# Renumbering the slots of the expert tables in a mixture-of-experts layer

## The chip, the cores and the metric

The kernel runs on one core of a Trainium2 chip. The metric is the device time of one execution, in microseconds (us); lower is better. The kernel before takes 911.71 us as the median of three runs (911.01 to 913.59). One execution was recorded by the hardware profiler; it took 911.96 us, and its span from the first to the last instruction is 909.6 us. A second measurement of this kernel would be told from no change at about 0.3%, that is 2.7 us.

The core has five engines that matter here. PE multiplies matrices, ACT (ScalarE) and DVE (VectorE) work element by element, POOL (GpSimd) issues the indirect transfers, and SP issues the plain transfers. All transfers are carried out by 16 DMA engines, whoever issues them.

## The reference

One decoder layer on 1024 tokens of width 1024: a layer norm, two kinds of attention side by side, an output projection, a layer norm, a mixture of experts, and a last layer norm. The change concerns the experts only.

```python
def hierarchical_moe(h, w_group, b_group, w_router, b_router, w_gate, w_up, w_down):
    ...
    g_top, g_idx = lax.top_k(group_probs, 1)          # 1 of 4 groups
    ...
    e_top, e_idx = lax.top_k(in_group, TOP_K)         # 2 of the 8 experts in it
    weights = g_top * jax.nn.softmax(e_top, axis=-1)
    expert_ids = g_idx * EXPERTS_PER_GROUP + e_idx
    ...
    hid = silu(xb @ w_gate[e]) * (xb @ w_up[e])       # 1024 -> 256
    hid = hid * combine
    out = sum over e of hid @ w_down[e]               # 256 -> 1024
```

Each token goes to two of 32 experts. An expert's weights are three blocks of 1 MB (gate, up and down, 128 partitions of 8 KB each).

## The kernel before

**The tables.** While the router runs, the kernel builds for each expert a list of its tokens. `route` (line 1475) counts with a triangular matrix how many earlier tokens chose the same expert; that count `pos` is the token's rank in the expert. Line 1529 compares `pos` with the row of constants `iota`, which gives a one-hot row of 128 columns, and the product in line 1533 puts the token's number into the list, on the partition whose `iota` equals the rank:

```python
                V.tensor_scalar(O, iota, pos[:, b, k:k + 1], None, op0=OP.is_equal)
                ...
                PE.matmul(flat(T), O, flat(Vk), start=(n == 0 and k == 0), stop=(n == NB - 1 and k == 1))
```

`finish_table` (line 1375) adds 4096 to each entry. An entry that holds a token becomes its number from 0 to 1023. An empty one becomes 4096, which is out of bounds for the indirect transfers, and they skip it. With `iota` equal to the column number, an expert with n tokens has its rows on partitions 0 to n-1. `overflow_table` (line 1820) uses the same `iota` for tokens of rank 128 and above, which go to an extra tile.

**The expert stage.** 33 tiles run one after the other (line 1878): 32 experts and, as tile 24, the overflow tile. The rows of each tile, counted by running the routing of the reference on its inputs, are in the order of the tiles 66, 74, 17, 76, 35, 58, 13, 55, 80, 79, 48, 22, 93, 123, 47, 67, 71, 62, 60, 25, 128, 121, 51, 68, 4 (overflow), 83, 96, 35, 70, 64, 93, 29, 35: 2048 rows of 4 KB in all. For each tile

- `gather_x` (line 1656) fetches its rows from the tensor `h_d` in device memory by an indirect DMA on POOL's queue (`w<-h_d,idx` in the trace), four tiles ahead;
- `load_chunk` (line 1328) fetches the three 1 MB blocks by plain DMAs on SP's queue (`rw<-in_w_e_dram`), each as soon as one of some ten buffers is free (`rw` has eight); tile 24 fetches its blocks by an indirect DMA;
- `w_split` (line 1551) turns each half block into a high and a low part, one operation on ACT (`whg`, `whd`) and one on DVE (`wlg`, `wld`), and so frees the buffer;
- PE transposes the rows (`x_tr`), multiplies (`gate_up`, `down`), and for tiles 0 to 30 `scatter` (line 1715) adds the result to the rows of `y_d` by an indirect DMA that accumulates (`y_d<-w,idx`).

All 128 rows of a tile are computed, whatever their number; an empty row holds old data and is multiplied by zero. After tile 30 all rows of `y_d` are read back for the last layer norm (`norm_rows`, `rw<-y_d`). Tiles 31 and 32 are not accumulated: their rows are fetched from `y_d` (`old_rows`, `w<-y_d,idx`), added, normalised and written into the output by an indirect DMA (`renorm`, `out_dram<-w,idx`), the last thing that the kernel does.

The order of all instructions is worked out ahead of time by a planner in the kernel (`Sched`, line 201), which knows shapes but not the numbers in a table.

Of the kernel before, what the change touches and what calls it, by code (L numbers as in the profile page):

```python
# [37 lines left out]
C_ID, C_TRI, C_IOTA, C_E32 = 0, 128, 256, 384  # L38
# [1932 lines left out]
def _constants():  # L1971
    import numpy as np
    c = np.zeros((128, C_END), np.float32)
    q = np.arange(128)[:, None]
    k = np.arange(128)[None, :]
    c[:, C_ID:C_ID + 128] = np.eye(128)
    cur = np.where(k <= q, 0.0, NEG)
    mask = np.concatenate([(k > q) & (k >= 128 - NMETA), cur, q > k, q <= k], axis=1).astype(np.float32)
    c[:, C_TRI:C_TRI + 128] = q < k
    c[:, C_IOTA:C_IOTA + 128] = k  # L1980
    col = np.arange(512)[None, :]
    bd = ((q[:64] // NMETA) == (col // 128)).astype(np.float32)
    c[:, C_E32:C_E32 + 32] = np.arange(32)
    J, e = np.divmod(np.arange(224), 32)
    key = np.zeros((128, 2, 7, 32), np.float32)
    key[:, 0] = (32 * (J + 1) + e).reshape(7, 32)
    key[:, 1] = (128 * (J + 1)).reshape(7, 32)
    c[:, C_TOK:C_TOK + 8] = np.arange(128)[:, None] + 128 * np.arange(8)[None, :] - EMPTY
    c[:, C_WROW] = 3 * np.arange(128)
    inv = 10000.0 ** (-np.arange(0, 64, 2, dtype=np.float32) / np.float32(64))  # L1990
    pos = np.zeros((128, 9), np.float32)
    pos[:, :8] = NMETA + 128 * np.arange(8)[None, :] + np.arange(128)[:, None]
    pos[:, 8] = np.maximum(np.arange(128) - (128 - NMETA), 0)
    ang = (pos[:, :, None] * inv.astype(np.float32)[None, None, :]).astype(np.float32)
    rope = np.zeros((128, 9, 2, 64), np.float32)
    rope[:, :, 0, :32] = rope[:, :, 0, 32:] = np.cos(ang)
    rope[:, :, 1, :32] = -np.sin(ang)
    rope[:, :, 1, 32:] = np.sin(ang)
    return c, rope, bd, key, mask
# [51 lines left out]
```

## Time and profile before

| | us |
|---|---|
| median of three runs | 911.71 |
| the profiled execution | 911.96 |
| its span, first to last instruction | 909.6 |
| first scatter to the last one (tiles 0 to 30) | 534.9 to 846.2 |
| PE busy in the span | 804.9 (88%) |
| DVE, ACT busy | 683.5 (75%), 512.9 (56%) |
| transfers on POOL's queue | 28.87 MB, 12816 packets |
| transfers on SP's queue | 166.41 MB, 36688 packets |

Up to about 505 us the kernel runs attention and the router, from there to about 846 us the expert stage, and then the tail with the last layer norm. In the views of DMA queues, q1 is SP's queue and q0 is POOL's; a share is the time that the queue's packets took, as a share of 16 DMA engines' time in the stretch. A row that a tile gathers or scatters is one packet of 4 KB, a row of a weight block one packet of 8 KB; very small packets go with them. "To landing" is the time from the issue of a transfer until all 16 DMA engines have reported that their part is done.

### The profile page before, as it was taken

What the parts mean: (1) busy time and instruction counts of PE and PEld (TensorE: products, weight loads), DVE (VectorE), ACT (ScalarE), POOL (GpSimd) and SP (SyncE); (2) the same over time, 40 slices, a digit from 0 to 9 for tenths busy, and PEclk for the clock granted to TensorE, in tenths of its full rate; (3) what the DMA queues carried; (4) which work ended last, traced back from release to release, by engine and by line L of the source; (5) the groups of instructions that cost most, each with busy time, mean ns of one, the idle gap of its engine ahead of it and who ended that gap; (6) DMA issues with size and microseconds to landing.
All of it is one profiled execution on the core that took longest, in us unless ns stands there. A gap on an engine that the chain in (4) does not pass through costs nothing. (4 is left out here: it accounts for less than half of the span.)

```text
span 909.6 us, 13571 instructions
## 1 busy us (share of the span) xinstructions
PE 804.9 (88%) x4616; PEld 688.2 (76%) x4616; DVE 683.5 (75%) x1379; ACT 512.9 (56%) x966; POOL 312.9 (34%) x561
## 2 busy tenths in 40 slices
PE   3899999999999999999998499999899989998520
PEld 3898998999999988888887388888677767765410
DVE  7946623888777655658667799998897779878595
ACT  3524322576665635512122598998787768768541
POOL 3757423344331215232214324343332243332100
PEclk9999999999999999999999699999999999999855
DMA  9544512121211112799957477999999999996632
GB/s 335 175 145 169 167 67 94 46 87 55 85 50 47 48 70 70 241 354 397 348 172 281 151 264 226 349 374 363 335 343 353 321 332 366 353 347 209 197 133 104
DMA packets 49574, 196.14 MB, mean 216 GB/s; under 512 B 12689, under 2 KB 14225, under 8 KB 37345
## 3 DMA queue, kind: packets, MB, share of 16 engines
q1 hardware_dynamic: 36688, 166.41, 49.3%
q0 software_dynamic: 12816, 28.87, 11.5%
q8 instruction: 37, 0.61, 0.3%
q14 instruction: 33, 0.26, 0.1%
HBM read 165.57 MB, written 49.05 MB: 236 GB/s over the span
## 5 line engine op out<-in xcount | busy, mean ns | idle before, releaser
L312 DVE TENSOR_TENSOR wlg<-rw,whg 128x1024 fp32r<-128x1024 f32 x120 | 143.3, 1220 | 32.4 <-ACT whg L312 32.1
L312 POOL DMA_INDIRECT y_d<-w,idx x33 | 72.4, 2193 | 224.6 <-ACT w L312 180.4
L312 ACT ACTIVATE whg<-rw 128x1024 fp32r<-128x1024 f32 x120 | 124.5, 1060 | 42.5 <-DMA rw<-in_w_e_dram 37.2
L312 PE MATMUL sc<-wh,ht 128*128 128x448 f32 (+3 forms) x400 | 116.2, 371 | 1.9 <-DVE ht L312 1.3
L312 PE MATMUL gu<-wlg,xh 128*128 128x512 f32 x264 | 106.3, 403 | 10.4 <-DVE wlg L312 10.4
L312 PE MATMUL gu<-whg,xh 128*128 128x512 f32 x264 | 109.3, 414 | 2.8 <-ACT whg L312 2.8
L312 PE MATMUL gu<-whg,xl 128*128 128x512 f32 x264 | 104.9, 398 | 2.1 <-DVE xl L312 2.1
L312 PEld LDWEIGHTS sc<-wh,ht 128*128 128x128 f32 x400 | 74.3, 192 | 9.5 <-DVE ht L312 1.8
L312 PE MATMUL sc<-wl,ht 128*128 128x448 f32 (+3 forms) x200 | 73.1, 365 | 0.0
L312 PEld LDWEIGHTS gu<-wlg,xh 128*128 128x128 f32 x264 | 49.9, 189 | 28.7 <-DVE wlg L312 18.1
L312 DVE TENSOR_TENSOR wld<-rw,whd 128x1024 fp32r<-128x1024 f32 x58 | 68.3, 1220 | 2.1 <-ACT whd L312 2.1
L312 PEld LDWEIGHTS gu<-whg,xh 128*128 128x128 f32 x264 | 50.0, 190 | 13.4 <-ACT whg L312 4.8
L312 PEld LDWEIGHTS gu<-whg,xl 128*128 128x128 f32 x264 | 50.2, 190 | 12.8 <-DVE xl L312 4.0
L312 ACT ACTIVATE whd<-rw 128x1024 fp32r<-128x1024 f32 x58 | 58.3, 1059 | 0.3 <-PE y L312 0.3
L312 PE MATMUL y<-whd,hh 128*128 128x512 f32 x124 | 51.3, 414 | 0.0
L312 PE MATMUL sc<-w,oT 128*128 128x512 f32 x192 | 49.8, 402 | 0.6 <-DMA oT<-o_d 0.6
L312 PE MATMUL tr<-cs,w 128*128 128x128 f32 x264 | 40.4, 277 | 10.9 <-DMA w<-h_d,idx 7.3
L312 DVE TENSOR_TENSOR xl<-tr,xh 128x512 fp32r<-128x512 f32 x66 | 45.2, 685 | 6.4 <-ACT xh L312 6.1
L312 ACT ACTIVATE pt<-sc,ng 128x272 f32<-128x272 f32 (+9 forms) x56 | 29.8, 538 | 34.5 <-DVE ng L312 34.3
L312 PE MATMUL y<-wld,hh 128*128 128x512 f32 x124 | 49.1, 396 | 0.0
L312 PE MATMUL y<-whd,hl 128*128 128x512 f32 x124 | 49.0, 395 | 0.0
L312 POOL DMA_INDIRECT w<-h_d,idx x33 | 44.1, 1337 | 11.2 <-issue 5.5
(331 smaller groups left out, 1961.3 us busy)
## 6 DMA issues: line engine op xcount, KB each, us to landing
rw<-in_w_e_dram SPq DMA_DIRECT2D x88, 1024.0 KB, 20.7
o_d<-oT SPq DMA_DIRECT2D x16, 512.0 KB, 2.7
oT<-o_d POOLq DMA_DIRECT2D x16, 512.0 KB, 8.5
x<-in_w_in_dram SPq DMA_DIRECT2D x8, 672.0 KB, 6.3
u_d<-r SPq DMA_DIRECT2D x7, 672.0 KB, 3.3
h_d<-h SPq DMA_DIRECT2D x8, 512.0 KB, 3.2
hr<-h_d SPq DMA_DIRECT2D x8, 512.0 KB, 9.7
h_d<-hr SPq DMA_DIRECT2D x8, 512.0 KB, 4.5
```

The costliest lines, as they stand in the source:

```text
L312: inst = getattr(t.eng.real, method)(*[self.real(a) for a in args], **{k: self.real(v) for k, v in kw.items()})
```

## The change

The row of constants `iota` gets other numbers. Column k held k; it now holds k % 8 * 16 + k // 8. So the token of rank r, which stood on partition r, stands on partition 8 * (r % 16) + r // 16: ranks 0 to 15 on partitions 0, 8, 16, ... 120, ranks 16 to 31 on partitions 1, 9, 17, ... 121, and so on. 64 rows, for example, stood on partitions 0 to 63 and stand now on those 64 partitions whose number leaves a remainder of 0 to 3 when divided by 8.

```diff
     c[:, C_TRI:C_TRI + 128] = q < k
-    c[:, C_IOTA:C_IOTA + 128] = k
+    c[:, C_IOTA:C_IOTA + 128] = k % 8 * 16 + k // 8
     col = np.arange(512)[None, :]
```

No instruction is added, removed or moved on any engine: the lists of PE, DVE, ACT, POOL and SP are row for row the same. What changes is data: which partitions of a tile hold rows, and so which of a gather's and a scatter's 128 places are skipped.

## Rows read from the trace of the kernel before

**Rows 1.** Stretches of the expert stage and the tail: length, then busy time (and instructions) of each engine, the granted clock of TensorE, the share of DMA engines and GB/s.

```profile
core 0: us, PE busy (x) PEld busy (x) DVE busy (x) ACT busy (x) POOL busy (x), PEclk, DMA share, GB/s
544.29:619.35 75.06, 75.06 (x370) 61.69 (x369) 73.01 (x83) 68.36 (x97) 29.36 (x17) 1.00 0.92 322
619.35:846.23 226.88, 208.29 (x979) 162.76 (x978) 190.22 (x233) 175.52 (x252) 74.61 (x42) 0.99 0.92 326
846.23:909.60 63.37, 13.25 (x48) 9.73 (x46) 43.08 (x93) 21.59 (x40) 8.01 (x7) 0.63 0.42 151
```

**Rows 2.** The scatters of the first stretch and of the second, POOL's instructions that touch `y_d`: count, shortest, median and longest in ns, first and last start.

```profile
L312 POOL DMA_INDIRECT y_d<-w,idx x9: 2135/2154/2159, 544.3 to 619.3; - x9
...
L312 POOL DMA_INDIRECT y_d<-w,idx x22: 1614/2340/3712, 619.3 to 846.2; - x22
```

**Rows 3.** Waits, longest first, of ACT from 540 to 620 us (first row), of ACT from 620 to 846 us (second row) and of PE from 620 to 846 us: us in total, times, longest.

```profile
ACT whg L312 <- PE gu L312: 4.5, 16, 0.3
...
ACT whg L312 <- DMA rw<-in_w_e_dram: 37.2, 21, 5.2
...
PE gu L312 <- DVE wlg L312: 10.4, 13, 2.2
PE gu L312 <- ACT whg L312: 2.8, 7, 0.8
```

**Rows 4.** Time to landing of the weight blocks (`rw`) that were issued from 540 to 620 us, from 620 to 730, from 730 to 790 and from 790 to 850.

```profile
DMA to landing us min/median/max: 4.7/10.7/23.3
...
DMA to landing us min/median/max: 18.9/22.4/25.1
...
DMA to landing us min/median/max: 12.3/19.0/23.4
...
DMA to landing us min/median/max: 18.1/24.0/26.2
```

**Rows 5.** The DMA engines in 40 slices of 0.05 us each, first from 900.3 to 902.3 us, when tile 31 writes its 29 rows into the output, then from 902 to 904 us, when tile 32 writes its 35 rows. GB/s counts a packet where it starts: 82 is one row of 4096 bytes in a slice, 492 is six.

```profile
GB/s 0 0 0 0 0 0 0 0 246 410 2 3 493 82 0 492 82 0 492 82 0 2 1 0 0 0 0 0 0 0 0 0 0 0 0 0 0 0 0 0
...
GB/s 0 0 0 0 0 0 0 0 492 164 3 84 492 82 82 492 82 82 492 82 0 84 1 0 82 0 0 82 0 0 0 0 0 0 0 0 0 0 0 0
```

**Rows 6.** What packets took, from the view of DMA queues: packets, MB, share of 16 engines. Both queues from 620 to 728 us; q1 from 526 to 534 us, when two weight blocks were loaded with nothing beside them; q0 from 854 to 868 us, when the 64 rows of `old_rows` were fetched.

```profile
q1 hardware_dynamic: 4293, 31.23, 75.3%
q0 software_dynamic: 2923, 5.61, 20.1%
...
q1 hardware_dynamic: 291, 2.12, 76.7%
...
q0 software_dynamic: 288, 0.26, 5.7%
```

**Rows 7.** The transfers between 563 and 850 us: weight blocks on SP's queue and by indirect DMA, scatters and gathers on POOL's: count, shortest, median and longest in ns, first and last start.

```profile
L312 SPq DMA_DIRECT2D rw<-in_w_e_dram x71: 327/328/743, 566.1 to 828.6; - x71
L312 POOL DMA_INDIRECT rw<-in_w_e_dram,widx x3: 988/1037/1732, 731.3 to 739.4; - x3
...
L312 POOL DMA_INDIRECT y_d<-w,idx x28: 1614/2284/3712, 563.1 to 846.2; - x28
L312 POOL DMA_INDIRECT w<-h_d,idx x24: 995/1232/2000, 565.5 to 804.9; - x24
```

**Rows 8.** The end of the program on POOL, in order of time: start, length, instruction, and in brackets what it had waited for.

```profile
899.20 0.97 POOL L312 DMA_INDIRECT out_dram<-w,idx  x1 [23.72 <-DVE z L312]
900.88 0.97 POOL L312 DMA_INDIRECT out_dram<-w,idx  x1 [0.71 <-DVEq L1942]
```

## Prediction

> **What bounds the kernel now.** I read the stretches of the expert stage first, then the waits in them, the landings of the weight blocks, and last the single packets. From 544.29 to 619.35 us PE is busy without a gap [rows 1], and nine scatters, one per tile, start in that stretch [rows 2]: eight intervals in 75.06 us, 9.38 us per tile. That is the pace when PE sets it. From 619.35 to 846.23 us 22 scatters start [rows 2]: 21 intervals in 226.88 us, 10.80 us per tile. At 9.38 us they would take 197.0 us, so this stretch loses 29.9 us. The waits say to whom: before 620 us ACT waited for PE only, after it for weight blocks, 37.2 us in 21 waits, and PE in turn for the halves that ACT and DVE split [rows 3]. And the blocks land late: the quickest of the first stretch in 4.7 us, in the second the median block in 22.4 us and even the quickest in 18.9 [rows 4]. A block is landed when the last of the 16 DMA engines is. So either all engines are behind, or a few.
>
> **Which engines carry the rows.** The last two transfers show it packet by packet [rows 5]. The 35 rows of tile 32 start as 6+2, 1+6+1, 1+6+1, 1+6+1, which is four rounds of eight, and then three single rows, one every three slices (0.15 us), the same beat as the rounds. So eight engines take four rows each and one of them takes three more, after its own four. Tile 31 with 29 rows starts 3+5, 6+1, 6+1, 6+1: a round of eight and three of seven, so seven engines with four rows and one with one. Only one simple dealing of partitions to engines gives both: partitions in groups of four, 0 to 3 to the first engine, and so on to the eighth, and partition 32 at the first again. Blocks of eight partitions per engine would show rounds of four or five; partition by partition round the 16 would show rounds of 16. That the upper 64 partitions are dealt in the same way to the other eight engines no row shows by itself; I assume it. [...]
>
> By this dealing the rows stand unevenly before. Call the engines of the lower half 0 to 7 and of the upper half 8 to 15. A tile with 64 rows puts eight on each of 0 to 7 and none on 8 to 15. Over all 33 gathers the counts for engines 0 to 15 are 237, 224, 224, 220, 208, 201, 191, 179, then 73, 61, 54, 47, 39, 36, 32, 22.
>
> **What a row costs.** From 620 to 728 us q1 took 75.3% of 16 x 108 us, 1301 us, for 31.23 MB, that is 3812 packets of 8 KB: 0.341 us each. q0 took 20.1%, 347 us, for 5.61 MB or 1370 rows: 0.253 us per row, gathers and scatters in equal parts, so 0.507 us for a pair [rows 6]. A plain row costs 5.7% of 16 x 14 us for 64 rows, 0.20 us [rows 6], which leaves 0.31 us for a row that is accumulated. Now engine 0 from 563.1 to 846.2 us, 283.1 us: 74 blocks [rows 7] of eight packets at 0.341 us are 201.9 us; the 28 scatters [rows 7], tiles 3 to 30, give it 206 rows, 63.9 us; the 24 gathers, tiles 9 to 32, give it 174 rows, 34.8 us. Sum 300.6 us, 6% more than there is, because the mean packet holds waits that a full engine doesn't have. Engine 0 is thus busy all the time. Engine 8 has 67 and 59 rows: 234.5 us, and idles a sixth. The few engines with the most rows are behind, and they set the landing of every block.
>
> **The change part by part.** The instructions stay; their number, order and shapes cost nothing either way. Only the rows' engines change. By the same dealing 64 rows now stand on the four lower partitions of every eight, which are the even groups of four: engines 0, 2, 4, ... 14 have eight rows each, the odd ones none. The crowd is moved, not thinned. A tile with 62 to 128 rows has eight on its fullest engine before and after. Small tiles gain, because 16 ranks are spread over eight engines before the next 16: 35 rows go from 7 to 5 on engine 0, 47 and 48 from 8 to 6, 51 from 8 to 7, 13 from 4 to 2, 17 from 4 to 3, the overflow's 4 rows from 4 to 1; 22, 25 and 29 stay at 4, 55 to 60 at 8. All gathers together then give the even engines 220, 219, 218, 213, 207, 204, 202, 201 rows, and the odd ones 54 to 36.
>
> In the stretch where engine 0 is always busy its scatters go from 206 rows to 192 (tiles 4, 6, 10, 14 and 27 save two each, 22 one, 24 three), and its gathers from 174 to 162 (10, 14, 27 and 32 two each, 22 one, 24 three). 14 x 0.31 + 12 x 0.20 = 6.7 us; scaled by 283.1/300.6, as its packets are quicker than the mean, 6.4 us. It stays the fullest after the change (engine 2 has 192 and 162 too). Since it sets the pace for 29.9 us more than PE needs, the saving reaches the end in full.
>
> After the change four engines lie within one row of engine 0's scatters (192, 192, 191, and 187) where before the next had ten fewer (196). A block now waits for the last of several equals. No row prices that; it lies between nothing and the whole 6.4 us, and I take 1 us, nearer to nothing, because a packet that is late on one engine is made good by the next ones. In the tail the last transfer [rows 8] has five rows on its fullest engine, not seven: 2 x 0.15 us [rows 5], 0.3 us off the landing after the last instruction. From 544 us to 563 us nothing is gained, as PE has no gap there [rows 1], and the first gather of the stage (66 rows) has eight rows on its fullest engine before and after.
>
> Sum: -6.4 + 1.0 - 0.3 = -5.7 us on the profiled 911.96 us, 906.3 us. That run lies 0.25 us above the median, so 906.0 us.
>
> **Rivals.**
>
> *The rows are not what makes the blocks late.* The core moves 326 GB/s in the second stretch at a mean DMA share of 0.92 [rows 1]; if a common limit holds all engines back, it doesn't matter which carry the rows: 911.7 us. For it: the share is high on the mean of 16 engines, though the sum above leaves half of them a sixth idle. Against it: the first stretch moves 322 GB/s at the same share and PE waits for nothing, and with two blocks alone a packet took 76.7% of 16 x 8 us over 259 packets, 0.379 us [rows 6], so 0.341 us among gathers is not slow. [...]
>
> *Slower: two full engines side by side.* Before, each of the full engines 0 to 7 writes partitions p while its partner of the upper half, p + 64, has few rows. Now 0 and 8, 2 and 10, 4 and 12, 6 and 14 are full together. If such a pair shares a path, its load decides: packets 2 x 201.9 us, rows 98.7 + 32.6 before, and after the change 91.9 for engine 0 and 181 x 0.31 + 154 x 0.20 = 86.9 for engine 8; 535.1 becomes 582.6, 9% more. The stretch from 619 us on would grow by 226.88 x 0.09 = 20 us: 932 us. It decides from where packets of the pairs take 0.0113 us (3%) longer: 24 packets per tile, 21 intervals and the 5.7 us. Against it: the two blocks loaded alone ran on all 16 engines at once with no more than 0.379 us a packet.
>
> *The rows spread over all 16.* If engines took blocks of eight partitions, 64 rows would give every engine four, half of before, and the whole 29.9 us could go: 882 us. Against it stand the three single rows of [rows 5].
>
> **How the numbers follow.** Forecast, 902 to 909 us: 0.60. No effect: 0.22. Slower: 0.13. Full spread: 0.05. A difference under 0.3% (2.7 us, so 909.0 to 914.4) can't be told from none. Faster: 0.60 of the forecast, less 0.02 for its upper edge, and 0.05, together 0.63; same: 0.22 and 0.02, 0.24; slower 0.13. The range that holds 8 in 10 leaves out the full spread and most of the slower case: 899 to 914 us. The forecast's own is 902 to 909 us, rounded outwards: 906.0 - 3.2 = 902.8 where the saved rows cost half as much again, 906.0 + 2.2 = 908.2 where the equals take back half of 6.4 us and not 1.
>
> **What would show it.** Right: the ACT waits for weight blocks fall from 37.2 us to about 31, the interval in the second stretch from 10.80 to about 10.5 us, the median block still lands in some 20 us, and the 35 rows of tile 32 start as four rounds of eight and then three rows that start together, not singly. Wrong: those rounds have 16 rows, or blocks land in 5 to 8 us (full spread); waits and landings stay as they are (no effect); packets of 8 KB take over 0.35 us in the second stretch (pairs).

## The result, and the profile after

The changed kernel takes 905.65 us (median of ten runs, 904.07 to 907.39), the kernel before 911.84 us in the same rounds. The ratio is 0.9934 with a 95% interval of 0.9919 to 0.9948: 6.2 us faster, where 5.7 us were forecast. The profiled execution took 904.6 us, its span is 902.3 us.

The stretches of the expert stage, cut as in [rows 1] at the start of the second, the tenth and the last scatter, and the scatters of the second stretch as in [rows 2]:

```profile
core 0: us, PE busy (x) PEld busy (x) DVE busy (x) ACT busy (x) POOL busy (x), PEclk, DMA share, GB/s
543.22:618.28 75.06, 75.06 (x370) 61.71 (x369) 72.98 (x83) 68.38 (x97) 29.37 (x17) 1.00 0.93 323
618.28:839.39 221.11, 205.73 (x979) 161.51 (x978) 189.90 (x233) 175.82 (x252) 71.42 (x42) 1.00 0.93 334
839.39:902.30 62.91, 13.13 (x48) 9.74 (x46) 43.08 (x93) 21.59 (x40) 8.01 (x7) 0.62 0.42 152
```

```profile
L312 POOL DMA_INDIRECT y_d<-w,idx x22: 1595/2304/2559, 618.3 to 839.4; - x22
```

The first stretch is what it was, 75.06 us. The second fell from 226.88 to 221.11 us, 5.8 us: 21 intervals of 10.53 us where there were 10.80. The tail fell from 63.37 to 62.91 us, 0.5 us. The remaining 1.1 us of the difference of the two spans lies before the expert stage begins (its first scatter starts at 533.8 instead of 534.9 us). It is there already when the first gather starts, at 506.9 instead of 507.9 us, before any row has gone through the changed table, so it is no work of the change; other runs of the study have 505.9 to 508.9 us there.

What ACT waited for from 620 to 840 us, as in [rows 3], and the landings of the blocks issued from 540 to 620 us and from 620 to 730 us, as in [rows 4]:

```profile
ACT whg L312 <- DMA rw<-in_w_e_dram: 30.2, 17, 4.6
```

```profile
DMA to landing us min/median/max: 4.8/9.1/19.7
...
DMA to landing us min/median/max: 12.0/21.7/24.0
```

The waits fell by 7 us, from 37.2 to 30.2. A second profile of the changed kernel, at nearly the same time (see the run with another engine full), has 24.2 us, so this sum tells the direction and not the size. The median block of the second stretch lands as late as before (21.7 us, 22.4 before). So engines are still behind; they are behind by a little less work.

Which engines, the 16 reports of a single block show. They are read from the trace's semaphore events, in us after the issue of the block; the first line is a block of the kernel before, issued at 706.67 us, the second one of the changed kernel, issued at 702.12 us:

```
before   5.2 5.2 5.2 5.2 5.2 5.2 5.2 5.3  6.3  7.7 11.9 15.2 20.9 20.9 22.1 22.9
changed  5.0 5.1 5.1 5.1 5.1 5.2 5.2 5.4 18.5 18.7 19.4 20.0 20.9 22.1 22.2 22.4
```

The reports don't name their engines; they are sorted by time. Before, eight are quick and the other eight are late in steps, four of them by some 16 us, which fits the eight uneven row counts from 237 down to 179. After, eight are quick and eight are late nearly alike, as the counts 220 to 201 are. And the 35 rows of tile 32, in slices of 0.05 us as in [rows 5] (894.9 to 896.9 us):

```profile
GB/s 0 0 0 0 0 0 0 0 328 84 247 247 164 164 164 246 246 82 328 246 82 246 0 0 1 0 0 0 0 0 0 0 0 0 0 0 0 0 0 0
```

The starts end with three rows in one slice (246), 13 slices after the first; before, three single rows followed each other and the last came 19 slices after the first. The tail's 0.3 us is there to be seen.

Where in the stage the time was saved, four scatters show, tiles 10 to 13, before and then after:

```profile
629.67 2.34 POOL L312 DMA_INDIRECT y_d<-w,idx  x1 [6.36 <-ACT w L312]
639.48 3.71 POOL L312 DMA_INDIRECT y_d<-w,idx  x1 [6.13 <-ACT w L312]
650.49 2.53 POOL L312 DMA_INDIRECT y_d<-w,idx  x1 [5.96 <-ACT w L312]
663.01 2.20 POOL L312 DMA_INDIRECT y_d<-w,idx  x1 [8.28 <-ACT w L312]
```

```profile
628.60 2.34 POOL L312 DMA_INDIRECT y_d<-w,idx  x1 [6.35 <-ACT w L312]
638.09 2.31 POOL L312 DMA_INDIRECT y_d<-w,idx  x1 [5.10 <-ACT w L312]
647.62 1.59 POOL L312 DMA_INDIRECT y_d<-w,idx  x1 [5.88 <-ACT w L312]
657.57 1.61 POOL L312 DMA_INDIRECT y_d<-w,idx  x1 [6.65 <-ACT w L312]
```

Three tiles took 33.3 us before and take 29.0 us now (29.1 in the second profile): 4.4 of the 5.8 us are won here. A reading that no run tests: the rows that tiles 4, 6 and 10 save on engine 0 were saved while the buffers still hid its backlog, and they pay out when the backlog reaches PE, from tile 10 on.

### The profile page after: what moved, and what is told of

Its sections match the earlier page's. It is cut to its first block, busy times and chain, and to the rows that moved or that the text cites. A ratio compares the mean times of both kernels' runs of the same rounds, so it can differ in the third digit from the quotient of the medians.

```text
span 902.3 us, 13571 instructions
## 1 busy us (share of the span) xinstructions
PE 801.0 (89%) x4616; PEld 685.7 (76%) x4616; DVE 683.2 (76%) x1379; ACT 513.3 (57%) x966; POOL 310.0 (34%) x561
## 5 line engine op out<-in xcount | busy, mean ns | idle before, releaser
L312 ACT ACTIVATE whg<-rw 128x1024 fp32r<-128x1024 f32 x120 | 124.5, 1061 | 36.4 <-DMA rw<-in_w_e_dram 30.2
L312 POOL DMA_INDIRECT y_d<-w,idx x33 | 67.8, 2056 | 219.9 <-ACT w L312 176.0
L312 PE MATMUL tr<-cs,w 128*128 128x128 f32 x264 | 40.4, 277 | 10.5 <-DMA w<-h_d,idx 7.2
L312 ACT ACTIVATE pt<-sc,ng 128x272 f32<-128x272 f32 (+9 forms) x56 | 29.9, 539 | 34.5 <-DVE ng L312 34.3
```

The costliest lines, as they stand in the source:

```text
L312: inst = getattr(t.eng.real, method)(*[self.real(a) for a in args], **{k: self.real(v) for k, v in kw.items()})
```

## The experiments

All layouts are made by the same line, with other numbers in `iota`. For a partition k, e is the DMA engine and s the place on it (0 to 7) by the dealing that the prediction read from the trace:

```diff
+    e, s = 8 * (k // 64) + k // 4 % 8, k % 4 + 4 * (k // 32 % 2)
```

**All 16 engines alike.**

```diff
-    c[:, C_IOTA:C_IOTA + 128] = k
+    c[:, C_IOTA:C_IOTA + 128] = 16 * s + e
```

> Rank r goes to DMA engine r % 16 of the dealing read from the trace, so 64 rows are four on each of 16 engines. Theory (the engine with the most rows sets the pace): from 563 us on the fullest engine has 125 scattered and 108 gathered rows where it had 206 and 174, 98.7 - 60.4 = 38 us less work, more than the 29.9 us that the second stretch lies above PE's pace; so nearly all of the 29.9 us goes, 880 to 886 us, intervals of the scatters 9.4 to 9.6 us, blocks landing in 5 to 10 us, ACT waits for weight blocks under 5 us. Rival (a limit that all engines share, so that it doesn't matter which carry the rows): 909 to 914 us, blocks landing in some 20 us. Rival (engines take blocks of eight partitions): this layout puts 64 rows four to an engine there too or worse, no gain over the changed kernel, 900 us or more.

Measured: 887.08 us, 24.5 us less than before (0.9725, 0.9709 to 0.9740). The second stretch, its scatters, and the landings of the blocks issued from 620 to 730 us:

```profile
617.02:821.93 204.91, 200.67 (x979) 162.09 (x978) 190.35 (x233) 175.86 (x252) 75.22 (x42) 1.00 0.97 359
```

```profile
L312 POOL DMA_INDIRECT y_d<-w,idx x22: 1595/2298/3504, 617.0 to 821.9; - x22
```

```profile
DMA to landing us min/median/max: 7.1/9.2/9.7
```

ACT's list of waits from 620 to 846 us no longer has a row for weight blocks, and a block lands in 9.2 us. Same instructions, same bytes, 22 us off the second stretch: which engines carry the rows is what made the blocks late. This refutes the rival of a limit common to all engines at 326 GB/s, since 359 GB/s are moved here, and it refutes blocks of eight partitions. It came out just above the forecast 880 to 886 us: 204.91 us is still 7.9 us over 21 x 9.38 us. PE itself is busy for 200.67 us of it, so about half of what is left is PE's own work; the 29.9 us were never all to be had. For 60 us of the stretch the mean share of the 16 engines is 1.02, at 385 GB/s:

```profile
620.00:680.00 60.00, 58.16 (x283) 46.73 (x282) 56.58 (x83) 50.78 (x73) 20.94 (x12) 1.00 1.02 385
```

From 730 to 790 us it moves 384 GB/s at the same share, 1.02. Why a block takes 9.2 us here, against some 5 us on a quick engine, no run shows.

**One full engine.**

```diff
+    c[:, C_IOTA:C_IOTA + 128] = np.where(e == 0, s, 7 + 15 * s + e)
```

> Ranks 0 to 7 all go to engine 0 and the others round the remaining 15, so that engine 0 has eight rows of every tile of eight rows or more and the other engines some four. Theory (the fullest engine alone sets the pace, because a block is landed when its last engine is): engine 0 has 220 scattered and 188 gathered rows from 563 us on where before had 206 and 174, 14 x 0.31 + 14 x 0.20 = 7.1 us, scaled 6.7 us more than before; 918 us, one engine landing some 20 us after the issue and 15 quick ones. Rival (the mean load, or the number of full engines, decides): near the even spread, 880 to 895 us.

Measured: 922.76 us, 11.2 us more than before (1.0120, 1.0101 to 1.0140). Fifteen engines carry 131 to 102 gathered rows over the stage and one 260, and the kernel is slower than with eight engines at 179 to 237. A block of this run, issued at 700.20 us, beside one of the even spread, issued at 708.41 us:

```
one full     4.6 4.7 4.7 4.7 4.7 4.8 4.9 4.9 4.9 5.0 5.0 5.0 5.3 5.5 6.7 22.7
even spread  4.6 4.7 4.7 4.8 4.8 4.9 5.0 5.0 5.1 5.1 5.2 5.2 6.0 6.1 6.6  7.1
```

One engine out of 16 makes every block late: of the plain blocks issued from 620 to 730 us the quickest lands in 21.5 us. The sign and the mechanism are the theory's; the size is 4.5 us above its 6.7 us.

**Full engines first.**

```diff
+    c[:, C_IOTA:C_IOTA + 128] = 8 * e + s
```

> Ranks 0 to 7 go to engine 0, 8 to 15 to engine 1, and so on: the tightest packing. The fullest engine has 220 scattered and 188 gathered rows from 563 us on, as in the run with one full engine, but the next ones have 253, 239, 222 gathered rows over the stage where that run has 131. Theory: 6.7 us more than before, 918 us, and the same as the run with one full engine; what it is above that run is what several nearly equal engines cost (forecast 1 us for the change). Rival (a shared limit): 912 us.

Measured: 921.50 us, 9.9 us more (1.0103, 1.0085 to 1.0120). It is 1.3 us below the run with one full engine, whose interval overlaps: engines that are nearly as full as the fullest cost nothing that can be seen here, and the 1 us that the prediction allowed for them is not seen. The size again exceeds the 6.7 us.

**The counts of before, on pairs.**

```diff
+    j = 2 * (e % 8) + e // 8
+    c[:, C_IOTA:C_IOTA + 128] = 64 * (j // 8) + 32 * (s // 4) + 4 * (j % 8) + s % 4
```

> The row counts of the kernel before, number for number, but on other engines: what engines 0 to 7 carried is carried by 0, 8, 1, 9, 2, 10, 3, 11, so that the full engines lie in pairs (partitions p and p + 64) as in the changed kernel. Theory: only the counts matter, 911.8 us like before (909 to 914.5). Rival (a pair shares a path): up to 20 us more, 932 us; anything from 915 us on speaks for it.

Measured: 911.88 us against 911.59, ratio 0.9999 (0.9987 to 1.0010). Moving the same counts to other engines changes nothing. The rival of the pairs falls, and the counts are what matters.

**Engine 0 as in the changed kernel, but alone.**

```diff
+    first = np.array([0, 16, 32, 48, 4, 20, 36, 52])
+    rest = np.setdiff1d(np.arange(128), first)
+    c[:, C_IOTA:C_IOTA + 128] = np.where(e == 0, first[s], rest[np.maximum(15 * s + e - 1, 0)])
```

> Engine 0 holds the very ranks that it holds in the changed kernel (0, 16, 32, 48, 4, 20, 36, 52), and all others go round the remaining 15 engines, so that it is full alone: 192 scattered and 162 gathered rows from 563 us on, the next engines about 118 and 100. It tells what the seven other full engines of the changed kernel cost. Theory with 1 us for several equals: 904.6 us. Theory in which the fullest engine alone counts: 905.6 us less nothing, the same as the changed kernel. Rival (the number of full engines or the mean load decides): 885 to 895 us.

Measured: 907.87 us against 912.31, 4.4 us less (0.9953, 0.9936 to 0.9970). The seven other full engines of the changed kernel are gone, and the time is not better but, if anything, 2 us worse. So the fullest engine decides, and taking its equals away gains nothing. As the rows are the same in number, the other 15 engines are busier instead (106 to 133 gathered rows, where half of them had 36 to 54); what that costs by itself this run does not separate.

**Ten engines.**

```diff
+    c[:, C_IOTA:C_IOTA + 128] = np.where(e < 10, 10 * s + e, 80 + 6 * s + e - 10)
```

> Ranks go round ten engines first: the fullest has 174 scattered and 147 gathered rows from 563 us on, halfway between the changed kernel (192 and 162) and the even spread (125 and 108). Theory (0.31 us for a scattered and 0.20 us for a gathered row of the fullest engine, times 0.94): 14.5 us less than before, 897.3 us (895 to 899). If the price per row is half as large or twice as large: 904 or 887 us.

Measured: 895.99 us against 912.31, 16.3 us less (0.9817, 0.9787 to 0.9846) where 14.5 were expected; it lies within the forecast 895 to 899. ACT's waits for blocks are 16.1 us, so blocks still hold the stage back. With the changed kernel (6.2 us for 14 scattered and 12 gathered rows) this makes two points on what the rows of the fullest engine cost.

**Scatters that don't add.**

```diff
-                             bounds_check=NB * 128 - 1, oob_is_err=False, compute_op=OP.add)
+                             bounds_check=NB * 128 - 1, oob_is_err=False)
```

> The layout of the kernel before; the scatters write their rows and do not add them to what is there, so the sum over experts is left out. It measures what the adding costs on the fullest engine. Theory: 206 rows x (0.31 - 0.20) x 0.94 = 21 us less than before, 890 us, if PE does not bind first (the even spread took 887.1 us). If a row that is added costs no more than a plain one: 911.6 us.

Measured: 890.74 us, 21.6 us less where 21 were expected (0.9761, 0.9737 to 0.9785). But this is no measure of the price. The second stretch:

```profile
620.45:825.47 205.02, 200.73 (x980) 162.08 (x979) 190.48 (x233) 175.92 (x252) 59.49 (x43) 1.00 0.91 356
```

That is the 204.91 us of the even spread, and ACT's waits are those of the even spread too (15.5 us for `y`, 9.6 us for `gu`, no row for weight blocks): PE and its order of instructions bind in both runs, as the expectation allowed for. So leaving out the adding frees at least 21.6 us, and that just 21 came out is luck.

The packets themselves give the price. The row of POOL's queue from 620 to 728 us, as in [rows 6]:

```profile
q0 software_dynamic: 3204, 6.31, 15.6%
```

It mixes rows with very small packets and with 71 packets of 8 KB of tile 24's blocks. Taken one by one from the trace, the 1397 packets of 4 KB took 0.161 us on the mean. In the kernel before, in the same window, the 4 KB packets fall into two groups with none between 0.2 and 0.32 us: 694 of 0.159 us and 673 of 0.330 us on the mean. Without adding, 1388 of the 1397 lie in the first group. So the packet of a plain row, gathered or written, took 0.16 us here and that of an added one 0.33 us, double.

**The key table earlier.** In the run with one full engine DVE waited once for a small table on SP's queue, by the author's reading behind the blocks of the full engine (620 us, from the waits of DVE):

```profile
DVE ovf L312 <- DMA kt<-in_c_key_dram: 4.0, 1, 4.0
```

That looked like the 4.5 us that the rows didn't explain, so the table was loaded nine tiles earlier.

```diff
     def overflow_list():
-        kt2 = pb.tile([128, 2, 7, NE], F32, name="kt2")
-        LD.dma_start(kt2, c_key)
+        kt2 = OV["key"]
...
+        if t == 3:
+            OV["key"] = pb.tile([128, 2, 7, NE], F32, name="kt2")
+            LD.dma_start(OV["key"], c_key)
         if t == 12:
             overflow_list()
```

> The layout with one full engine, and the table of the overflow keys (kt) is loaded in tile 3 and not in tile 12, when its part on the full engine stood behind the weight blocks and DVE waited 4.0 us for it. Theory: of the 11.2 us that this layout takes more than the kernel before, 6.7 us are the rows and 4 to 4.5 us this wait: 918 us. If the wait is absorbed by what comes after it: 922.8 us as without the edit.

Measured: 923.27 us against 912.31, 11.0 us more (1.0126, 1.0103 to 1.0148). The wait is gone from DVE's list, and the time stays. So the wait does not explain the 4.5 us.

**Another engine full.** The two layouts with engine 0 alone, with engines 0 and 12 exchanged.

```diff
     e, s = 8 * (k // 64) + k // 4 % 8, k % 4 + 4 * (k // 32 % 2)
+    e = np.where(e % 12 == 0, 12 - e, e)
```

> The layout with one full engine again, but it is engine 12 (partitions 80 to 83 and 112 to 115) that is full, and engine 0 has what engine 12 had, some 107 gathered rows in all. The run with engine 0 full took 11.2 us more than before where the rows' prices give 6.7. Theory A (engine 0 carries something besides rows and blocks, so that a crowd costs more there): 918 us or less. Theory B (all engines are alike, and the 4 us more come from being full earlier, before the blocks' buffers are used up): 922 to 923 us as with engine 0.

Measured: 927.06 us against 912.48, 14.6 us more (1.0158, 1.0139 to 1.0178).

> Engine 12 alone holds the ranks that engine 0 holds in the changed kernel. With engine 0 alone full it took 907.9 us, with eight engines full (the changed kernel) 905.65. Theory A (engine 0 carries something of its own): 904 us or less. Theory B (engines alike; one full engine and eight cost the same within the noise): 905 to 908 us.

Measured: 910.19 us against 912.48, 2.3 us less (0.9978, 0.9966 to 0.9991).

> The changed kernel on the same chip and in the same rounds as the run with engine 12 alone, for the comparison. 905.65 us. If several equally full engines cost 1 us, this is 1 us above the run with one of them alone; if they cost nothing, the two agree within 1 us.

Measured: 905.45 us, 7.0 us less (0.9932, 0.9917 to 0.9947). Its scatters run from 533.8 to 838.2 us, 304.4 us, where the first profile of the changed kernel has 305.6 and before 311.3.

Theory A falls: nothing of engine 0's own makes a crowd dearer there, it costs more on engine 12. Theory B falls in part. Eight full engines (905.45 us) are 4.7 us better than engine 12 alone with the same number of rows (910.19 us), on the same chip. And on engine 12 either layout takes more, against the kernel before on the same chip, than on engine 0: 14.6 and 11.2 us more for the one, 2.3 and 4.4 us less for the other. The runs with engine 0 were on two other chips, so that engine and chip are not told apart; against the chip speaks only that engine 0 full took 11.2 us more on one of the two and 11.0 (with the table earlier) on the other. Why engine 12 is dearer, no run here tells. Exactly one report is late when partitions 80 to 83 and 112 to 115 are the crowded ones, so one engine serves these eight: in the run with engine 12 alone the block issued at 707.07 us has 15 reports by 5.3 us and the last at 22.7.

## Why the prediction was right, and where not

**What bounds the kernel**: right. The even spread took ACT's waits for weight blocks away and 22 us out of the second stretch, and one full engine among 16 brought all of it back.

**Which engines carry the rows**: right. The dealing in groups of four, read from three late single rows, built layouts that do what they should: the even spread, ten engines, and a single engine, 0 or 12, on which every block waits. The assumption that the upper 64 partitions are dealt alike to the other eight engines was only assumed; the changed kernel's own eight equally late engines and the run with engine 12 bear it out. The runs also show that engines whose places are mostly skipped don't hold a block up: in the two blocks above eight of 16 report within 5.4 us.

**What a row costs**: the pair was right, its two parts were not. Packet by packet a plain row took 0.16 us and an added one 0.33, where the prediction had 0.20 and 0.31; its 0.20 had put 224 very small packets and one slow row on 64 rows. For 14 and 12 rows the errors cancel: 6.5 us against 6.7. Nor was the scaling needed: a packet of 8 KB took 0.309 us on the median from 620 to 728 us before, and with these three prices engine 0's sum is 279 of 283.1 us, and engine 8, by the same estimate, idles a quarter, not a sixth. The run without adding shows how the split could have misled: by the packets the adding is worth 206 x 0.17 = 35 us on the fullest engine, an estimate, not 21, and only PE's pace kept the gain at 21.6. For less work the sum of prices held: 6.2 us measured for 6.4 to 6.7, and 16.3 for 14.5 with ten engines. For more work it was too small: 11.2 and 9.9 us where 6.7 were forecast. The later wait of DVE was tried as the cause and is none; that the lone engine is dearer than one among eight may be part of it, but eight full engines first gave 9.9 us too. This stays open.

**The sum**: the 6.4 us of the stretch came out as 5.8 us in one profile and, as first to last scatter, 6.9 us in the other; the 0.3 us of the tail as 0.5 and 0.4. The step that failed is the 1 us for "the last of several equals": engine 0 alone is not quicker (907.87 us) than eight equals (905.65), so no such cost is seen, and if anything the sign is the other; nor does a run show that a late packet is made good by the next ones, the reason given for taking so little. (Of the four that the prediction put within one row, three are, at 192, 192 and 191; the fourth has 187.) Without the term the sum is 6.7 us, which lies between the two measurements, 6.2 and 7.0 us. "The saving reaches the end in full" holds, but not the reason that 29.9 us stood ready: with the even spread, and again without adding, the stretch still takes 205 us, so some 22 us did.

**The signs named ahead**: ACT's waits 30.2 us (about 31 said; the second profile's 24.2 makes the closeness luck), interval 10.53 us and 10.47 in the second profile (about 10.5), median landing 21.7 us (some 20), three rows that start together at the end of tile 32. The rivals gave none of their signs: blocks land as late as before, and a layout with full pairs costs nothing.

## What to carry to other kernels

Each weight block here landed with the last of its 16 reports; with one full engine 15 came by 6.7 us and the last at 22.7 us. So the indirect transfers that loaded a few engines delayed the blocks behind them (the median block of 620 to 730 us landed in 22.4 us before, in 9.2 us with the even spread), and the mean share of the engines didn't tell: it was 0.92 before, in the stretch without waits for blocks and in the one with them. Put row r of a list on a partition of engine r % 16: here `iota = 16 * s + e` gives 887.1 us, 2.7% less than before and about 2% less than the change, with not one instruction altered. Spreading by a step of eight partitions looks even and isn't (905.65 us); the starts of the packets, in slices of 0.05 us here, tell which partitions share an engine.

## What the runs showed of the hardware that was not expected

The packet of a row that is added to device memory took 0.33 us, that of a plain one 0.16 us, on the mean from 620 to 728 us; leaving out the adding gained 21.6 us here, in a stretch of 205 us that PE's pace sets with the even spread too. And engine 12 full, with 15 lighter ones beside it, takes 4.7 us more than eight equally full engines on the same chip (910.19 us against 905.45). With engine 0 it is some 2 us (907.87 against 905.65, each against the kernel before of its own rounds), with intervals that overlap. The cause of that is open.
